# A hybrid attention block on one core: order of loading the first value weights, order of the late value tiles, and place of three steps of the state chains

## The chip, the core and the metric

The kernel runs on one core of one Trainium2 chip. A core has five engines with queues of their own: TensorE (PE; its weight loads are listed apart, as PEld), VectorE (DVE), ScalarE (ACT), GpSimd (POOL) and SyncE (SP), which here only issues DMAs. The metric is the device time of one execution in microseconds; a time is the median over the runs.

## The reference

One layer of a bidirectional hybrid encoder on x of 1024 tokens by 1024 features, in float32:

```python
h = rmsnorm(x, norm_mix)
q, k, v, r, lr_f, lr_b, u, g_a, g_b = jnp.split(h @ w_in, split_points, axis=-1)
log_a_f = jax.nn.log_sigmoid(lr_f @ w_decay_up_fwd + b_decay_fwd) / 16      # log_a_b alike
o = gla_chunked(q, k, v, log_a_f, True) + flip(gla_chunked(flip(q), flip(k), flip(v), flip(log_a_b), False))
o = per_head_rmsnorm(o) * gla_norm * silu(r)
y_a = o @ w_branch_gla
y_b = pooled(u) @ w_pool_group * pool_scale
x = x + (sigmoid(g_a) * y_a + sigmoid(g_b) * y_b) @ w_out
x = x + swiglu(rmsnorm(x, norm_ffn)) ; out = rmsnorm(x, norm_final)
```

The gated linear attention has 4 heads with keys of 128 and values of 256 columns. In each direction a state of 128 x 256 runs over the chunks of tokens: `S_t = diag(alpha_t) S_(t-1) + k_t^T v_t`. This recurrence is the chain that the change touches; the other part of the change is at the start, where x is normalized and the first products with `w_in` are made.

## The kernel before

**Products.** Float32 operands are split into a high part (a cast to fp32r on ScalarE) and a low part (a subtraction on VectorE or GpSimd; `split_to`, L196 to L198). A product of two split operands is three matmuls: high with high, high with low, low with high (`products`, L268; all its matmuls are listed under L271). `mm3` (L273) is such a product followed by `pump`, which advances work that runs beside.

**Work beside.** The order of all engines' instructions is the order in which the program emits them; each engine takes its own in that order. Side work is written as generators in the list `side`; `begin(gen, delay)` (L186) appends one. `pump(dt)` (L158) takes `dt` from the first generator's delay (1 for an `mm3` of 512 columns, 0.5 for one of 256) and advances it when the delay is spent; a `yield d` in it means "after d more". Only the first generator of the list advances. `finish_side` (L189) drains the list at once. `pending` holds splits of weights, `take` (L256) hands out the next projection weights and `prepare` (L248) starts the splits of those after; `prepare_beside` paces a second list of side work.

**Memory.** `slot()` gives one of 39 slots of 128 x 1024 float32. The pool `wts` has a tag `raw` with four buffers for weights as they are loaded. Five PSUM banks (`ps_g`) serve transposes and attention, three (`ps_mm`) the main products. A tile that is given a buffer waits until the former tile's readers are done.

**Start.** SyncE issues the loads of x tiles 0 and 1, small vectors, four of the eight weight tiles of the values of heads 0 and 1 ("pair weights", `vraw`, each 128 x 512), x tiles 2 and 3, and the low-rank weights (`lraw`). The other four pair weights are issued by `split_pair_weight` (L368), each when the split before has freed a buffer. `norm_x(t)` (L390) normalizes tile t (a Square with a sum on ScalarE, the power on GpSimd, the scaling on VectorE) and issues the load of tile t + 4 into the same slot. `to_features` (L332) transposes two tiles on TensorE and splits them into `hT` (hh and hl). `pair_products(ts)` (L439) makes the values of heads 0 and 1 for token tiles ts; the first call, for tiles 0 and 1, is interleaved with `first_steps(k)` (L452), which splits the weights for step k + 1, transposes and norms. Tiles 2 and 3 follow, with norms and transposes of tiles 4 and 5 beside, then `first_qk` (L887): the low-rank product (`low_rank`, L479), q and k of head 0, with norms and transposes of tiles 6 and 7 beside. Values of tiles 4, 5 and then 6 with 7 are made after `begin(attention(0, ...))` (L909), so beside the attention of head 0.

**Attention of a head** (generator `attention`, L665), beside the products of what comes next. For each half of the tokens and each direction: `decay` sums the logarithms (VectorE, with a scan), `exponentials` (ScalarE, three Exp), `apply_decay` (ke on VectorE, qe and a factor on GpSimd). `transposed_keys` (L748) transposes ke on TensorE and splits it into kt. The backward chain (L814 to L830) goes over the eight chunks from the last down: `advance` (L756) makes kv = k^T v on TensorE (three matmuls), the new state st = kv * factor + old on VectorE, and the next step's old state so = st * factor on VectorE; then ScalarE writes the state for this chunk's output, sb. Chunks 7 to 4 use kt of the upper half, 3 to 1 that of the lower. `scores(0)` (sc) follows, then the forward chain (L836 to L863): per chunk the output op from scores and values, from qe and sb, and from qe and sf (ScalarE's scaled state), with `advance` between. `while h not in v_heads` (L805) holds the chain until the values of the head are made.

Of the kernel before, what the change touches and what calls it, by code (L numbers as in the profile page):

```python
# [10 lines left out]
F32 = mybir.dt.float32  # L11
# [3 lines left out]
AF = mybir.ActivationFunctionType  # L15
ALU = mybir.AluOpType

P = 128
D = 1024
SEQ = 1024  # L20
KT = D // P
NT = SEQ // P
HALF = 512
HEADS = 4
DK = 128
DV = 256
# [25 lines left out]
def kernel(  # L52
# [38 lines left out]
    def name(s):  # L91
        count[0] += 1
        return f"{s}_{count[0]}"
# [92 lines left out]
    def begin(gen, delay=0.0):  # L186
        side.append([gen, delay])

    def finish_side():  # L189
        while side:  # L190
            for _ in side[0][0]:
                pass
            side.pop(0)


    def split_to(hi, lo, src, eng=nc.vector):  # L196
        nc.scalar.copy(hi, src)  # L197
        eng.tensor_tensor(lo, src, as_f32(hi), op=ALU.subtract)  # L198
# [133 lines left out]
    def to_features(xn, t0, act, gain):  # L332

        for kp in range(KT // 2):
            ps = bank(ps_g, "tr")
            for i in range(2):
                transpose_tile(ps, xn[i], i, kp)
            gain_and_split(ps, kp, t0, act, gain)
            yield 1
# [10 lines left out]
    def load_x(t):  # L350
        nc.sync.dma_start(xt[t % 4][:, :], x[t * P : (t + 1) * P, :])
# [7 lines left out]

    pair_raw, pair_w = [], []  # L360

    def load_pair_weight():
        k = len(pair_raw)
        raw = wts.tile([P, HALF], F32, tag="raw", name=name("vraw"), bufs=4)
        nc.sync.dma_start(raw[:, :], w_in[k * P : (k + 1) * P, V0 : V0 + 2 * DV])
        pair_raw.append(raw)

    def split_pair_weight():  # L368
        k = len(pair_w)
        w = slot(F32R, s="wv")  # L370
        pair_w.append((w[:, 0, :], w[:, 1, :]))
        split_to(*pair_w[k], pair_raw[k][:, :], (nc.vector, nc.gpsimd)[k % 2])
        if len(pair_raw) < KT:
            load_pair_weight()

    load_x(0)
    load_rows(0, *vec_rows[0])
    load_x(1)
    for i in range(1, len(vec_rows)):
        load_rows(sum(n for _, n in vec_rows[:i]), *vec_rows[i])  # L380
    for _ in range(4):
        load_pair_weight()
    for t in (2, 3):
        load_x(t)
    nc.sync.dma_start(lraw[:, :, :], w_in[:, LR0:U0].rearrange("(k p) c -> p k c", p=P))
    nc.gpsimd.memset(uraw[:, :, :, :], 0.0)

# [8 lines left out]
    def norms(t0):  # L396
        for t in (t0, t0 + 1):
            norm_x(t)
            yield 2
# [13 lines left out]
    def low_rank_weights():  # L413
        for i in range(2):
            raw = lraw[:, 4 * i : 4 * i + 4, :]
            nc.scalar.copy(lw[i][:, :, :3, :], raw.unsqueeze(2).broadcast_to([P, 4, 3, 2 * RANK]))
            nc.vector.tensor_tensor(lw[i][:, :, 3, :], raw, as_f32(lw[i][:, :, 0, :]), op=ALU.subtract)
        nc.scalar.copy(up[:, :, :, :], uraw[:, :, :, :])
        nc.vector.tensor_tensor(up[32:64], uraw[32:64], as_f32(up[32:64]), op=ALU.subtract)
# [19 lines left out]
    def pair_products(ts, before=None):  # L439
        banks = [bank(ps_mm) for _ in ts]  # L440
        for k in range(KT):
            if before:
                before(k)
            for ps, t in zip(banks, ts):
                mm3(ps[:, :], tokens(hT(k, t // 4), t), pair_w[k], k == 0, k == KT - 1)
        for ps, t in zip(banks, ts):
            for h in range(2):
                if t % 4 == 0:
                    pair_v[h].append((slot(F32R, (4, DV), "vh"), slot(F32R, (4, DV), "vl")))
                split_to(*(part[:, t % 4, :] for part in pair_v[h][t // 4]), ps[:, h * DV : (h + 1) * DV])  # L450

# [18 lines left out]
    pair_products((2,))  # L470
    finish_side()
    begin(to_features(xn, 4, hT, g_mix), 1)
    low_rank_weights()
    prepare()
    pair_products((3,))
    finish_side()
    lrT = slot(F32R, (2, HALF), "lrT")

    def low_rank(half):  # L479
# [185 lines left out]
    def attention(h, q, k):  # L665
# [71 lines left out]
        def factor(n, d, which):  # L737
            f = fac[n // 4, d]
            i = n % 4
            if which == "whole":  # L740
                return f[:, 8 + i : 9 + i]
            first_half = (which == "before") == (d == 0)
            return f[:, 2 * i : 2 * i + 1] if first_half else f[:, 2 * i + 1 : 2 * i + 2]
# [9 lines left out]
            split_to(kt[:, 0, :], kt[:, 1, :], kp[:, :])  # L753
            return kt

        def advance(old, n, d, kt):  # L756

            kv = bank(ps_g, "kv")
            products(kv[:, :DV], tokens((kt[:, 0, :], kt[:, 1, :]), n), value(n))
            new = s1((DV,), "st")[:, :]  # L760
            after = factor(n, d, "after")
            if old is None:
                nc.vector.tensor_scalar(new, kv[:, :DV], after, None, op0=ALU.mult)
            else:
                nc.vector.scalar_tensor_tensor(
                    new, kv[:, :DV], after, old[:, :], op0=ALU.mult, op1=ALU.add
                )
            following = n + 1 if d == 0 else n - 1
            old = s1((DV,), "so")
            nc.vector.tensor_scalar(old[:, :], new, factor(following, d, "whole"), None, op0=ALU.mult)  # L770
            return new, old

        def scores(half):
            sc = [bank(ps_g, "sc") for _ in range(2)]
# [26 lines left out]
        yield 1.5  # L801
        apply_decay(0, 0)
        decay(1, 0)
        yield HOLD
        while h not in v_heads:  # L805
            yield 0.5
        v = v_heads[h]
# [4 lines left out]
        sb = [slot(shape=(4, DV), s="sb") for _ in range(2)]  # L812
        old = None
        for n in range(NT - 1, 0, -1):  # L814
            state, old = advance(old, n, 1, kts[n // 4, 1])
            m = n - 1
            nc.scalar.activation(
                sb[m // 4][:, m % 4, :], state, AF.Copy, scale=factor(m, 1, "before")
            )
            if n == 7:  # L820
                exponentials(1, 0)
            elif n == 5:
                apply_decay(1, 0)
            yield 1.2
            if n == 7:
                kts[0, 1] = transposed_keys(0, 1)
                yield 0.5
            if n == 2:
                kts[0, 0] = transposed_keys(0, 0)
                yield 0.5  # L830
# [5 lines left out]
        for n in range(NT):  # L836
            half, i = n // 4, n % 4
            op = bank(ps_g, "op")
            products(op[:, :DV], tokens(p, n), value(n), last=False)
            terms = []  # L840
            if n < NT - 1:
                terms.append((chunk_of(qe, n, 1), sb[half][:, i, :]))
            if n > 0:
                terms.append((chunk_of(qe, n, 0), sf[:, :]))
            for j, (a, b) in enumerate(terms):
                if j == len(terms) - 1 and n < NT - 1:
                    state, old = advance(old, n, 0, kts[half, 0])
                    sf = s1((DV,), "sf")
                    nc.scalar.activation(sf[:, :], state, AF.Copy, scale=factor(n + 1, 0, "before"))
                nc.tensor.matmul(op[:, :DV], a, b, start=False, stop=j == len(terms) - 1)  # L850
            nc.vector.tensor_copy(o[half][:, i, :], op[:, :DV])
            nc.scalar.activation(
                op[:, DV:], op[:, :DV], AF.Square, scale=1.0 / 16.0, accum_out=ms[:, n : n + 1]
            )
            if n == 0:
                yield 0.38
                kts[1, 0] = transposed_keys(1, 0)
            if n == 1:
                yield 0.75
                q_next = scores(1)  # L860
            if n == 3:
                p = q_next
            yield 1.02  # L863
# [22 lines left out]

    def first_qk():  # L887
        q, k = slot(s="q"), slot(s="k")
        begin(norms(6), 1)
        low_rank(0)  # L890
        weights = [take()]
        begin(to_features(xn[2:], 6, hT, g_mix), 1)
        for half in range(2):
            if half:
                finish_side()
                low_rank(1)
                prepare()
            for n, (dst, scale) in enumerate(((q, DK**-0.5), (k, 1.0))):
                if n == len(weights):
                    weights.append(take(ahead=False))  # L900
                ps = feature_major(weights[n], hT, half)
                nc.scalar.activation(dst[:, half, :], ps[:, :], AF.Copy, scale=scale)
        return q, k

    for h in range(HEADS):
        qk = project_qk() if h else first_qk()
        begin(attention(h, *qk))
        if h == 0:
            for ts in ((4,), (5,), (6, 7)):  # L909
                pair_products(ts)  # L910
            v_heads.update(enumerate(pair_v))
            prepare_beside(map(branch_jobs, range(4)), 5)
        if h > 1:
            v = value_slots()
            w = take()
            for t in range(NT):
                values(w, v, t)
            v_heads[h] = v
# [1009 lines left out]
```

## Time and profile before

| what | us |
|---|---|
| median of 3 runs (lowest, highest) | 1404.41 (1403.36, 1405.44) |
| the profiled execution, its own time | 1404.11 |
| its span, first to last instruction | 1402.4 |
| TensorE busy | 1367.1 |
| VectorE, GpSimd, ScalarE busy | 857.7, 744.3, 624.6 |
| mean granted TensorE clock | 0.998 |

In a timeline row stand: start and duration in us, engine, line, operation, written tile, then the tiles read, shapes, the count of merged instructions, and in brackets the idle time of the engine before it with what ended that idle time. A row of waits has the total, the number and the longest of them. In a group of instructions stand the count, the busy time, the mean in ns, and the idle time before them. TensorE's durations overlap in a row of matmuls; its pace is read from the starts. Rows of SPq are DMAs as they are issued, not as they land.

### The profile page before, as it was taken

What the parts mean: (1) busy time and instruction counts of PE and PEld (TensorE: products, weight loads), DVE (VectorE), ACT (ScalarE), POOL (GpSimd) and SP (SyncE); (2) the same over time, 40 slices, a digit from 0 to 9 for tenths busy, and PEclk for the clock granted to TensorE, in tenths of its full rate; (3) what the DMA queues carried; (4) which work ended last, traced back from release to release, by engine and by line L of the source; (5) the groups of instructions that cost most, each with busy time, mean ns of one, the idle gap of its engine ahead of it and who ended that gap; (6) DMA issues with size and microseconds to landing.
All of it is one profiled execution on the core that took longest, in us unless ns stands there. A gap on an engine that the chain in (4) does not pass through costs nothing. (4 is left out here: it accounts for less than half of the span.)

```text
span 1402.4 us, 18182 instructions
## 1 busy us (share of the span) xinstructions
PE 1367.1 (97%) x6485; PEld 1143.3 (82%) x6485; DVE 857.7 (61%) x1076; ACT 624.6 (45%) x1119; POOL 744.3 (53%) x555
## 2 busy tenths in 40 slices
PE   6999999999999999999999999999999999999997
PEld 5778898988888878788887888888888888888876
DVE  5456667676934975577884865656555556343363
ACT  5545646554433444455346633333333334453253
POOL 3212526242279455567666076667666667464354
PEclk9999999999999999999999999999999999999999
DMA  6111324132469757997524555554444447976451
GB/s 214 39 45 49 115 63 143 52 121 61 135 188 279 223 194 231 347 405 264 182 88 161 183 182 173 173 172 149 138 149 148 139 155 254 386 258 222 166 229 72
DMA packets 166588, 243.61 MB, mean 174 GB/s; under 512 B 10937, under 2 KB 95969, under 8 KB 166497
## 3 DMA queue, kind: packets, MB, share of 16 engines
q1 hardware_dynamic: 166496, 242.45, 51.5%
q8 instruction: 51, 0.84, 0.3%
q14 instruction: 41, 0.33, 0.1%
HBM read 164.55 MB, written 77.86 MB: 173 GB/s over the span
## 5 line engine op out<-in xcount | busy, mean ns | idle before, releaser
L198 POOL TENSOR_TENSOR wl<-fs,wh 128x512 fp32r<-128x512 f32 x120 | 166.0, 1387 | 164.3 <-ACT wh L197 139.0
L271 PE MATMUL ps<-gl,wh 128*128 128x512 f32 x616 | 239.8, 389 | 0.9 <-DVE gl L1520 0.9
L271 PE MATMUL ps<-gh,wh 128*128 128x512 f32 x616 | 240.3, 390 | 0.0
L271 PE MATMUL ps<-gh,wl 128*128 128x512 f32 x616 | 239.7, 389 | 0.0
L198 POOL TENSOR_TENSOR wl<-fraw,wh 128x512 fp32r<-128x512 f32 x90 | 129.6, 1441 | 64.8 <-ACT wh L197 64.7
L271 PE MATMUL ps<-hh,wh 128*128 128x512 f32 x376 | 151.6, 403 | 0.0
L198 POOL TENSOR_TENSOR ol<-gor,oh 128x1024 fp32r<-128x1024 f32 (+1 forms) x42 | 100.0, 2386 | 93.2 <-ACT oh L197 76.0
L271 PE MATMUL ps<-hh,wl 128*128 128x512 f32 x376 | 146.7, 390 | 0.0
L271 PE MATMUL ps<-hl,wh 128*128 128x512 f32 x376 | 146.5, 390 | 0.0
L271 PEld LDWEIGHTS ps<-gl,wh 128*128 128x128 f32 x616 | 115.6, 188 | 25.0 <-DVE gl L1520 1.3
L271 PEld LDWEIGHTS ps<-gh,wl 128*128 128x128 f32 x616 | 115.6, 188 | 24.2
L271 PEld LDWEIGHTS ps<-gh,wh 128*128 128x128 f32 x616 | 115.6, 188 | 23.6
L198 POOL TENSOR_TENSOR wl<-raw,wh 128x512 fp32r<-128x512 f32 x40 | 54.4, 1370 | 129.5 <-ACT wh L197 119.1
L271 PE MATMUL ps<-oh,oh 128*128 128x512 f32 x308 | 119.9, 389 | 1.0 <-DVE x L1850 1.0
L271 PE MATMUL ps<-ol,oh 128*128 128x512 f32 x308 | 120.0, 389 | 0.2 <-DVE ol L198 0.2
L271 PE MATMUL ps<-oh,ol 128*128 128x512 f32 x308 | 119.8, 389 | 0.0
L198 POOL TENSOR_TENSOR wl<-wraw,wh 128x512 fp32r<-128x512 f32 x56 | 89.6, 1629 | 45.3 <-ACT wh L197 45.2
L198 DVE TENSOR_TENSOR ol<-wor,oh 128x1024 fp32r<-128x1024 f32 (+1 forms) x42 | 62.0, 1496 | 53.6 <-ACT oh L197 46.3
L197 ACT CAST wh<-fs 128x512 fp32r<-128x512 f32 x120 | 73.7, 615 | 28.3 <-DVE fs L940 28.2
L271 PEld LDWEIGHTS ps<-hh,wl 128*128 128x128 f32 x376 | 70.6, 188 | 15.1
L271 PEld LDWEIGHTS ps<-hl,wh 128*128 128x128 f32 x376 | 70.8, 188 | 13.0
L271 PEld LDWEIGHTS ps<-hh,wh 128*128 128x128 f32 x376 | 70.7, 188 | 13.0
(259 smaller groups left out, 3115.1 us busy)
## 6 DMA issues: line engine op xcount, KB each, us to landing
fraw<-in_w_ffn_in_dram SPq DMA_DIRECT2D x44, 512.0 KB, 5.8
gor<-g_out SPq DMA_DIRECT2D x35, 512.0 KB, 5.5
g_out<-s SPq DMA_DIRECT2D x44, 256.0 KB, 2.3
raw<-in_w_in_dram SPq DMA_DIRECT2D x40, 256.0 KB, 5.2
fraw<-in_w_in_dram SPq DMA_DIRECT2D x20, 512.0 KB, 6.6
wor<-t_out SPq DMA_DIRECT2D x20, 512.0 KB
g_out<-g SPq DMA_DIRECT2D x33, 256.0 KB, 3.2
x<-in_x_dram SPq DMA_DIRECT2D x16, 512.0 KB, 4.9
```

The costliest lines, as they stand in the source:

```text
L197: nc.scalar.copy(hi, src)
L198: eng.tensor_tensor(lo, src, as_f32(hi), op=ALU.subtract)
L271: nc.tensor.matmul(ps, a[i], b[j], start=first and n == 0, stop=last and n == 2, skip_group_check=onto)
```

## The change

All eight pair weights are loaded ahead, two to a slot, between x tiles 2 and 3 and after; the chained loads of `split_pair_weight` go. Norms and transposes of tiles 6 and 7 are begun ahead of the fourth pair product rather than in `first_qk`, and the drain behind that product goes. Late values are made in the order 7, 6, then 5 with 4. In `attention`, the transposed keys of the lower half backward and the exponentials of the upper half forward move from the chain's first step to 2.5 ahead of it, and that half's `apply_decay` from the third step of the chain to its first. `advance` scales both the state for the output and the old state on ScalarE, in this order.

```diff
-    def load_pair_weight():
-        k = len(pair_raw)
-        raw = wts.tile([P, HALF], F32, tag="raw", name=name("vraw"), bufs=4)
-        nc.sync.dma_start(raw[:, :], w_in[k * P : (k + 1) * P, V0 : V0 + 2 * DV])
-        pair_raw.append(raw)
+    def load_pair_weights():
+        raw = slot(s="vraw")
+        for i in range(2):
+            k = len(pair_raw)
+            nc.sync.dma_start(raw[:, i, :], w_in[k * P : (k + 1) * P, V0 : V0 + 2 * DV])
+            pair_raw.append(raw[:, i, :])
...
-        split_to(*pair_w[k], pair_raw[k][:, :], (nc.vector, nc.gpsimd)[k % 2])
-        if len(pair_raw) < KT:
-            load_pair_weight()
+        split_to(*pair_w[k], pair_raw[k], (nc.vector, nc.gpsimd)[k % 2])
...
-    for _ in range(4):
-        load_pair_weight()
-    for t in (2, 3):
-        load_x(t)
+    load_pair_weights()
+    load_pair_weights()
+    load_x(2)
+    load_pair_weights()
+    load_x(3)
+    load_pair_weights()
...
-                if t % 4 == 0:
+                if t // 4 == len(pair_v[h]):
...
     begin(to_features(xn, 4, hT, g_mix), 1)
+    begin(norms(6), 0.5)
+    begin(to_features(xn[2:], 6, hT, g_mix), 2)
     low_rank_weights()
     prepare()
     pair_products((3,))
-    finish_side()
...
-        def advance(old, n, d, kt):
+        def advance(old, n, d, kt, dst):
...
-            nc.vector.tensor_scalar(old[:, :], new, factor(following, d, "whole"), None, op0=ALU.mult)
-            return new, old
+            nc.scalar.activation(dst, new, AF.Copy, scale=factor(following, d, "before"))
+            nc.scalar.activation(old[:, :], new, AF.Copy, scale=factor(following, d, "whole"))
+            return old
...
-        yield HOLD
+        yield HOLD - 2
+        kts[0, 1] = transposed_keys(0, 1)
+        exponentials(1, 0)
+        yield 2.5
...
-            state, old = advance(old, n, 1, kts[n // 4, 1])
             m = n - 1
-            nc.scalar.activation(
-                sb[m // 4][:, m % 4, :], state, AF.Copy, scale=factor(m, 1, "before")
-            )
+            old = advance(old, n, 1, kts[n // 4, 1], sb[m // 4][:, m % 4, :])
             if n == 7:
-                exponentials(1, 0)
-            elif n == 5:
                 apply_decay(1, 0)
             yield 1.2
-            if n == 7:
-                kts[0, 1] = transposed_keys(0, 1)
-                yield 0.5
...
-                    state, old = advance(old, n, 0, kts[half, 0])
                     sf = s1((DV,), "sf")
-                    nc.scalar.activation(sf[:, :], state, AF.Copy, scale=factor(n + 1, 0, "before"))
+                    old = advance(old, n, 0, kts[half, 0], sf[:, :])
...
-        begin(norms(6), 1)
         low_rank(0)
         weights = [take()]
-        begin(to_features(xn[2:], 6, hT, g_mix), 1)
...
-            for ts in ((4,), (5,), (6, 7)):
+            for ts in ((7,), (6,), (5, 4)):
                 pair_products(ts)
```

`HOLD` is 4.4.

## The prediction

> **What bounds the kernel now.** I read the page's busy line first, then the waits of TensorE over the whole span, then busy times by stretch, and last the timeline round the few waits that the change can reach.
>
> ```profile
> PE 1367.1 (97%) x6485; PEld 1143.3 (82%) x6485; DVE 857.7 (61%) x1076; ACT 624.6 (45%) x1119; POOL 744.3 (53%) x555
> ```
>
> TensorE sets the time. The other engines cost time only where TensorE waits, so the change is worth the waits that it ends less those it starts. TensorE's waits, longest first:
>
> ```profile
> PE vps L427 <- DMA rows<-in_b_decay_bwd_dram: 6.7, 1, 6.7
> PE ps L271 <- ACT hh L325: 3.8, 1, 3.8
> PE kv L271 <- DVE kt L198: 3.7, 3, 1.4
> PE tr L318 <- DVE xn L307: 2.4, 3, 1.1
> ...
> PE kv L271 <- ACT vh L197: 1.9, 1, 1.9
> ```
>
> The first is the start of the program and stays. The other four, 11.8 us, lie in the stretch that is edited. Busy times in three stretches (us and, after PEclk, granted clock, DMA share, GB/s) show what else is lost:
>
> ```profile
> core 0: us, PE busy (x) PEld busy (x) DVE busy (x) ACT busy (x) POOL busy (x), PEclk, DMA share, GB/s
> 10.00:20.00 10.00, 6.66 (x29) 5.30 (x27) 3.72 (x6) 4.40 (x11) 2.58 (x2) 1.00 0.87 308
> 20.00:30.00 10.00, 8.63 (x37) 6.76 (x38) 5.87 (x13) 6.30 (x16) 4.35 (x4) 0.83 0.60 168
> 900.00:1000.00 100.00, 100.00 (x443) 82.81 (x442) 51.94 (x56) 35.65 (x64) 63.82 (x47) 1.00 0.47 151
> ```
>
> Undisturbed, 443 matmuls of 512 columns take 100 us: 0.226 us each, though each is listed as 0.39 because they overlap. Right after the long wait the granted clock is 0.83 over 10 us, which is 1.7 us of clock lost.
>
> **Part 1: the pair weights.** The start in order of time:
>
> ```profile
> 6.56 0.90 SPq L351 DMA_DIRECT2D x<-in_x_dram  x2
> 7.51 0.43 SPq L385 DMA_DIRECT2D lraw<-in_w_in_dram  x1
> 8.07 2.51 SPq L351 DMA_DIRECT2D x<-in_x_dram  x2
> 10.57 1.09 PE L271 MATMUL ps<-wv,hh 128*128 128x512 f32 x2
> 10.68 3.83 SPq L365 DMA_DIRECT2D vraw<-in_w_in_dram  x4
> 12.16 0.63 ACT L197 CAST wv<-vraw 128x512 fp32r<-128x512 f32 x1
> 16.27 0.39 PE L271 MATMUL ps<-wv,hl 128*128 128x512 f32 x1
> 18.39 0.62 ACT L197 CAST wv<-vraw 128x512 fp32r<-128x512 f32 x1 [5.60 <-DMA vraw<-in_w_in_dram]
> 20.47 0.73 PE L271 MATMUL ps<-wv,hh 128*128 128x512 f32 x2 [3.81 <-ACT hh L325]
> 22.10 0.80 PE L271 MATMUL ps<-wv,hl 128*128 128x512 f32 x1 [0.90 <-DVE hl L328]
> ...
> 26.56 0.60 PE L318 MATMUL tr<-ident,xn 128*128 128x128 f32 x4
> 26.91 0.71 PE L271 MATMUL ps<-wv,hh 128*128 128x512 f32 x2
> ...
> 30.31 0.70 PE L271 MATMUL ps<-wv,hh 128*128 128x512 f32 x2
> ```
>
> TensorE's 3.81 us are named after ScalarE's hh, but ScalarE itself stood 5.60 us for the fifth weight: its load was issued at 10.68, behind four tiles of x and lraw. In the change x3, lraw, x4 and x5 come behind it: 3 x 128 x 1024 x 4 B and 1024 x 32 x 4 B, 1.70 MB fewer ahead. At the 308 GB/s of that stretch this is 5.5 us, so the weight lands at 18.4 - 5.5 = 12.9, as ScalarE finishes the fourth cast (12.16 + 0.63 = 12.8). From there ScalarE's work runs on without a stop while TensorE has matmuls until 16.5.
>
> How early can the eight steps end? They are 8 x 2 x 3 = 48 matmuls, 10.9 us, plus four groups of transposes at 26.91 - 26.56 = 0.35, 1.4 us: begun at 10.57, they end at 22.9 at best, where now the next product starts at 30.31. 7.4 us are lost: 3.81 + 0.90 idle, most of the 1.7 of clock, the rest small. I take **6.5 us**, leaving 0.9 for the norms of x2 and x3, which now come closer on TensorE's heels (cover: the four steps until 16.5; without it each late norm shows as a wait for hh or hl). Bounds: 3.8 (only the wait for the load goes, and the following steps stay limited by ScalarE and VectorE) to 7.4. SyncE issues the four loads 0.45 us apart (0.90 / 2); x4 and x5 move behind them and are read only after the first product, lraw later still. The weights leave the pool of four raw buffers for four of 39 slots, free at the start, so q's first weights find their buffers free; were slots short, a later tile would wait for a split that is long done.
>
> [...]
>
> **Part 2: norms of tiles 6 and 7 and their transposes earlier.** Of the waits for xn, tile 5's is not touched; tile 7's is:
>
> ```profile
> 44.19 0.67 ACT L197 CAST wh<-raw 128x512 fp32r<-128x512 f32 x1
> ...
> 44.89 0.39 PE L483 MATMUL ps<-hh,lw 128*128 128x512 f32 x1
> ...
> 46.22 1.06 ACT L311 ACTIVATE xn<-x 128x1024 f32<-128x1024 f32 x1
> 49.20 0.38 PE L318 MATMUL tr<-ident,xn 128*128 128x128 f32 x2
> 50.63 0.44 PE L318 MATMUL tr<-ident,xn 128*128 128x128 f32 x2 [1.06 <-DVE xn L307]
> ```
>
> The low-rank product begins at 44.89; its eight pairs take 2 x 0.226 = 0.45 us and count 2/3 each. Before, the norms come with its second and fifth pair, the transposes one product of 0.68 after its last: 49.20. Now the norms come with the sixth and eighth product of the fourth pair product (two products, and none, ahead of 44.89), the transposes with its sixth or seventh pair: norms 2.3 us sooner, transposes 1.1 to 1.6 (47.6 to 48.1 of this clock). ScalarE is busy with earlier work until about 44.9, so the Square starts 1.3 us sooner than 46.22, not 2.3, and the transposes may overtake that. With the transposes 1.1 sooner the wait shrinks a little, with 1.6 it grows by 0.3; but tile 6's norm then no longer shares VectorE with the split of the low-rank result. I take **0.6** (bounds -0.5 and 1.1, the whole wait). The removed drain after the fourth product emptied an almost empty list: nothing.
>
> **Part 3: value tiles 7, 6, 5, 4; keys and exponentials ahead of the chain.** Each head's chain stalls once; the four stalls, and what stands in front of head 1's:
>
> ```profile
> 104.27 0.38 PE L271 MATMUL kv<-vh,kt 128*128 128x256 f32 x1 [1.92 <-ACT vh L197]
> 172.00 0.48 DVE L763 TENSOR_SCALAR st<-kv,fac 128x256 f32<-128x256 f32 x1
> 172.57 0.51 ACT L817 ACTIVATE sb<-st,fac 128x256 f32<-128x256 f32 x1 [4.34 <-DVE st L763]
> 172.59 1.47 DVE L770 TENSOR_SCALAR so<-st,fac 128x256 f32<-128x256 f32 x1
> 175.20 0.69 DVE L198 TENSOR_TENSOR kt<-kp,kt 128x512 fp32r<-128x512 f32 x1 [1.14 <-ACT kt L197]
> 175.95 0.39 PE L271 MATMUL kv<-vh,kt 128*128 128x256 f32 x1 [1.42 <-DVE kt L198]
> 180.78 2.16 PE L778 MATMUL sc<-qe,ke 128*128 128x128 f32 x16
> 240.07 0.39 PE L271 MATMUL kv<-vh,kt 128*128 128x256 f32 x1 [1.20 <-DVE kt L198]
> 302.83 0.39 PE L271 MATMUL kv<-vh,kt 128*128 128x256 f32 x1 [1.06 <-DVE kt L198]
> ```
>
> Head 0's chain starts with tile 7, which is split last; turned round, tile 7 is split two products before. The 1.92 goes. In heads 1 to 3, kt of the lower half is wanted at the fifth step, and its cast on ScalarE stands behind exponentials that stand behind the first sb, which waited 4.34 us for VectorE. Ahead of the chain the cast no longer waits for st; its subtraction follows the decay on VectorE, which ends by 172.0, so kt is there at about 172.8, wanted at 175.95 - 1.42 = 174.5. The 1.42 + 1.20 + 1.06 = 3.68 go. The exponentials now make ScalarE wait for the decay, but it waited there for st anyway; value casts queue behind them as before. Yields: 4.4 + 0.5 become 2.4 + 2.5, so the chain's place does not move.
>
> **Part 4: the old state on ScalarE.** 56 instructions move:
>
> ```profile
> L770 DVE TENSOR_SCALAR so<-st,fac 128x256 f32<-128x256 f32 x56 | 28.2, 504 | 3.7
> ```
>
> On ScalarE such a scaling takes 0.51 (sb above): it gains 56 x 0.51 = 28.6 us, VectorE loses 28.2. A link of the chain was st 0.48 (172.00 above) + so 0.50 = 0.98 (up to 0.48 + 1.47 = 1.95); it becomes st 0.48 + dst 0.51 + old 0.51 = 1.5, with casts in between more. TensorE notices through the banks: I count that sc's second bank is the one of the fifth state. Head 1: st7 172.8, fifth state ready 4 x 1.5 + 0.5 later, 179.3; sc wants the bank halfway through its 2.16, at 180.78 - 1.42 + 1.0 = 180.4. Slack 1 us; about none in heads 2, 3 and 0, where links ran shorter. So I give back 0.4 in head 0 and 0.8 in the others together: **1.5 and 2.9 us** (bounds 0 to 1.9 and -3, one bank wait of 2 us a head over the gain, to 3.7).
>
> [...]
>
> Sum: 6.5 + 0.6 + 1.5 + 2.9 = **11.5 us** off the profiled execution's 1404.11 (its span 1402.4 and 1.7 round it), 1392.6. That execution lies 0.3 below the median of 1404.41, so the forecast is **1393**, its own range 1390 to 1396.
>
> **Rivals.**
> (A) ScalarE's chain becomes the bound: sc or the first op waits in each head. For it: the link of 1.5; against it: st starts sooner than now. The 4.4 us of parts 3 and 4 go and some 1.5 more: 1404.4 - 7.1 + 1.5 = 1399. Chance 0.17.
> (B) ScalarE, not the load, paces the start: x3 lands behind two weights, its norm is late, and 3.8 remain of 6.5: 1396. Chance 0.10.
> (C) The change doesn't do what it says: the fifth weight is still last, since all lie in one queue: part 1 falls away, 1399.5. The order of issue speaks against it. 0.04.
> (D) Slower. The forward chain:
>
> ```profile
> 201.36 0.51 ACT L849 ACTIVATE sf<-st,fac 128x256 f32<-128x256 f32 x1 [1.20 <-DVE st L765]
> 202.82 0.59 PE L850 MATMUL op<-sf,qe 128*128 128x256 f32 x2
> ```
>
> sf is ready 0.95 before its matmul. If queued work on ScalarE (the old state, a square, a cast) makes it 1.5 late, each of 28 steps (7 a head) waits 0.55, 15.4 us: 1393 + 15 = 1408. It decides from 0.95 + 11.5 / 28 = 1.36 us of lateness on. Against it: ScalarE idles 1.20 before sf, more than the 0.51 added. 0.04.
>
> **How the numbers follow.** Forecast 0.65, the four rivals 0.35. The range 1389 to 1399.5 runs from all waits gone (7.4 + 1.1 + 1.9 + 3.7 = 14.1, rounded out) through B and most of A. Faster by over 0.2% (below 1401.6): 0.92; within 0.2%, about what this kernel's measurement cannot tell from none: 0.03; slower: 0.05.
>
> **What would show it.** Part 1: no wait over 1 us between 10 and 25, clock 1.00 there, the third product starting near 24. Part 2: the wait on xn under 1.06 near 42. Parts 3 and 4: no kv wait for vh or kt; instead at most short waits of sc or op on st or p. A wait of op for sf, or of sc in every head, would make the forecast wrong; so would casts of weights that still wait for DMA.

## The result and the profile after

| | before | changed |
|---|---|---|
| median (lowest, highest), 6 runs each, us | 1403.17 (1402.41, 1405.44) | 1395.54 (1394.44, 1396.57) |
| ratio, 95% interval | | 0.9943 (0.993 to 0.9955) |
| profiled execution, its own time | 1404.11 | 1395.00 |
| its span | 1402.4 | 1393.0 |

The change makes the kernel 7.6 us faster by the medians, 9.1 by the two profiled executions. The forecast was 1393. What the median gains depends on the kernel before, which scatters: of its 36 executions recorded beside the experiments, the 14 with a mean granted clock of 0.997 or 0.998 took 1401.6 to 1405.7 us, the other 22 (0.995 or 0.996) 1404.0 to 1408.5, while the changed kernel's twelve (0.998 or 0.999) took 1394.4 to 1396.6. Where the changed kernel was run once more (e9 below), the difference of the medians was 10.5.

The busy line of the page of the changed kernel:

```profile
PE 1366.3 (98%) x6485; PEld 1143.3 (82%) x6485; DVE 830.7 (60%) x1020; ACT 643.6 (46%) x1175; POOL 743.6 (53%) x555
```

VectorE lost 27 us, ScalarE got 19; neither is what the time is made of. TensorE's longest waits in the first 400 us:

```profile
PE vps L428 <- DMA rows<-in_b_decay_bwd_dram: 6.8, 1, 6.8
PE tr L318 <- DVE xn L307: 1.9, 3, 1.0
PE op L271 <- ACT p L197: 1.2, 2, 0.6
PE op L271 <- DVE p L198: 0.9, 4, 0.2
```

The waits for hh (3.8), hl (0.9), kt (3.7) and vh (1.9) of before are gone; those of op for p, 2.1 together (0.2 in before), stand in their place. The two stretches of the start, with the columns shown for before:

```profile
10.00:20.00 10.00, 10.00 (x41) 8.28 (x40) 7.25 (x14) 8.57 (x19) 5.92 (x6) 1.00 1.02 350
20.00:30.00 10.00, 10.00 (x54) 8.34 (x53) 5.84 (x15) 6.08 (x15) 1.16 (x2) 1.00 0.61 171
```

TensorE is busy throughout, with 41 and 54 matmuls where there were 29 and 37. The timeline of the start:

```profile
10.64 1.20 PE L271 MATMUL ps<-wv,hh 128*128 128x512 f32 x2
12.07 1.05 PE L271 MATMUL ps<-wv,hh 128*128 128x512 f32 x2
13.34 0.63 PE L271 MATMUL ps<-wv,hh 128*128 128x512 f32 x2
13.42 0.62 ACT L197 CAST wv<-vraw 128x512 fp32r<-128x512 f32 x1 [0.56 <-DMA vraw<-in_w_in_dram]
...
20.86 0.60 PE L318 MATMUL tr<-ident,xn 128*128 128x128 f32 x4
...
39.16 0.39 PE L485 MATMUL ps<-hh,lw 128*128 128x512 f32 x1
43.47 0.44 PE L318 MATMUL tr<-ident,xn 128*128 128x128 f32 x2 [0.74 <-DVE xn L307]
```

The fifth cast comes at 13.42 (before at 18.39), after 0.56 us of waiting for its load. The transposes ahead of the third pair product start at 20.86 instead of 26.56, the low-rank product at 39.16 instead of 44.89.

To see where the gain arises, the starts of the same matmuls in both traces are set against each other; each row is the difference of this trace or that of an experiment below to the profiled execution of before, in us, at the transposes of the third product (26.56 in before), the first product behind both low-rank halves (z, 77.67), the last op of head 0 (139.26) and of head 3 (332.05), and the end of the last matmul (1395.63):

| kernel | third product | behind low-rank | end of head 0 | end of head 3 | last matmul |
|---|---|---|---|---|---|
| changed | -5.70 | -6.03 | -7.65 | -9.20 | -9.38 |
| changed, second trace (e9) | -5.52 | -5.84 | -7.44 | -8.87 | -8.65 |
| loads alone (e4) | -6.07 | -6.08 | -6.05 | -6.73 | -5.03 |
| tile order alone (e5) | -0.82 | -0.81 | +0.21 | -0.19 | -0.43 |
| keys and exponentials alone (e6) | +0.06 | +0.06 | -0.43 | -4.49 | -4.68 |
| old state on ScalarE alone (e3) | -1.15 | -1.15 | -0.79 | +2.04 | +3.06 |
| changed, old state on VectorE (e1) | -5.86 | -6.18 | -8.16 | -11.62 | -12.15 |
| changed, old state first on ScalarE (e2) | -5.67 | -5.98 | -8.60 | -12.96 | -12.49 |
| e2 with later transposes (e7) | -4.98 | -6.75 | -9.37 | -14.01 | -14.24 |
| e7 with a later norm (e10) | -6.48 | -7.88 | -10.49 | -15.30 | -15.18 |
| weights ahead of x (e8) | -4.61 | -4.91 | -6.54 | -7.51 | -6.53 |

So the change won 5.7 in the start, 0.3 behind it, 1.6 in head 0 and 1.55 in heads 1 to 3; the forecast had 6.5, 0.6, 1.5 and 2.9. Each trace is one execution, so differences of some tenths between them mean little: e4 gains 0.68 in heads 1 to 3, where it has no edit. In e3, e4 and e8 some 0.7 to 0.9 us are lost late, between 526 and 759, where nothing was edited: TensorE waits there for the load of ph, 1.8, 0.7 and 0.6 us, which it does not in the trace of before. In e4 a further 0.8 goes near the end.

### The profile page after: what moved, and what is told of

Same layout as the page of the kernel before. It is cut to its first block, busy times and chain, and to the rows that moved or that the text cites. A ratio compares the mean times of both kernels' runs of the same rounds, so it can differ in the third digit from the quotient of the medians.

```text
span 1393.0 us, 18153 instructions
## 1 busy us (share of the span) xinstructions
PE 1366.3 (98%) x6485; PEld 1143.3 (82%) x6485; DVE 830.7 (60%) x1020; ACT 643.6 (46%) x1175; POOL 743.6 (53%) x555
```

## The experiments

Each run's ratio, and what it is said to be below the kernel before by the medians, goes by executions of the kernel before on the same chip.

**The theory after the result.** The waits that the forecast named are the ones that went; heads 1 to 3 gave back more than forecast because the old state sits on ScalarE behind the output's state (a longer link). Rivals: the new order of keys and exponentials itself costs; or the old state on ScalarE costs as such, wherever it stands in its queue. For the start: the half pace of the first matmuls, or the norms that are now close on TensorE's heels.

**Loads alone (e4_only_loads).** The kernel before with the new order of loads:

```diff
-    for _ in range(4):
-        load_pair_weight()
-    for t in (2, 3):
-        load_x(t)
+    load_pair_weights()
+    load_pair_weights()
+    load_x(2)
+    load_pair_weights()
+    load_x(3)
+    load_pair_weights()
```

> The kernel before with only the loads of the pair weights as in the change (all ahead, two to a slot). Theory: the third pair product starts 5.7 us sooner, near 24.6 instead of 30.31, and all of it arrives: 1397 to 1398. Of the 6.5 expected 0.9 is lost since TensorE's clock is at half until 13.3 us here and until 11.4 in the trace of before: where that edge falls elsewhere, the start moves by half of its shift. Rival: the start's gain is partly lost behind, norms of tiles 4 to 7 on TensorE's heels: under 5 us, 1399.

Measured: 1399.88 us, ratio 0.996 (0.9946 to 0.9973), 5.7 below the kernel before by the medians, as its theory had it. The start gains 6.07, and the heads keep their waits. Part 1 stands alone: it does not need the other parts.

**Tile order alone (e5_only_tiles).** The kernel before with:

```diff
-                if t % 4 == 0:
+                if t // 4 == len(pair_v[h]):
...
-            for ts in ((4,), (5,), (6, 7)):
+            for ts in ((7,), (6,), (5, 4)):
```

> The kernel before with one edit: the late value tiles of a head are made in the order 7, 6, then 5 with 4. Theory (as predicted): the wait of kv for vh in head 0, 1.92 us, goes and nothing takes its place, so 1.5 to 2 us less than the kernel before; the three waits of kv for kt (3.7 together), the start and heads 1 to 3 stay as they are. Rival: the chain that is let go earlier in head 0 stops at another place (an op or sc that waits for values or for p), and less than 0.7 us is left of it.

Measured: 1404.03 us, ratio 0.9987 (0.9978 to 0.9997), 1.8 below the kernel before by the medians (0.4 to 3.1 by the interval). That is the size that the theory gave, but its reason fails: something does take the wait's place. The rival's short gain is what the profiled execution shows (0.43 at the last matmul), at a place that the rival did not name. The waits of kv, and the timeline of head 0's chain:

```profile
PE kv L271 <- DVE kt L198: 5.0, 4, 1.8
```

```profile
105.28 0.51 ACT L817 ACTIVATE sb<-st,fac 128x256 f32<-128x256 f32 x1 [0.94 <-DVE st L763]
...
106.18 0.59 ACT L724 ACTIVATE z<-z 128x512 f32<-128x512 f32 x1
...
107.29 0.58 ACT L197 CAST kt<-kp 128x512 fp32r<-128x512 f32 x1
...
108.65 0.39 PE L271 MATMUL kv<-vh,kt 128*128 128x256 f32 x1 [1.80 <-DVE kt L198]
```

Four waits for kt instead of three: the wait for vh is gone (none is listed), and head 0 now stops at the fifth step, as heads 1 to 3 do, for the kt whose cast stands behind sb and the exponentials. In before, head 0 did not show that wait because it had already stood for vh: there this kt was ready at 109.40 and wanted at 110.12. The wait of 1.80 was also followed by 3.41 us at half clock (last section), so this execution loses 1.02 in head 0. Whether the edit pays by itself stays open between the medians and this trace; its wait is gone for good only together with the next edit.

**Keys and exponentials alone (e6_only_ahead).** The kernel before, with the old state left on VectorE and:

```diff
-        yield HOLD
+        yield HOLD - 2
+        kts[0, 1] = transposed_keys(0, 1)
+        exponentials(1, 0)
+        yield 2.5
...
-                exponentials(1, 0)
-            elif n == 5:
                 apply_decay(1, 0)
...
-            if n == 7:
-                kts[0, 1] = transposed_keys(0, 1)
-                yield 0.5
```

> The kernel before with one edit: transposed keys of the lower half backward and exponentials of the upper half forward ahead of the chain, that half's decay at the first step; the old state stays on VectorE. Theory: the three waits of kv for kt, 3.7 us, go without anything in their place, so 3.0 to 3.7 us less than the kernel before, all of it in heads 1 to 3 (about 1.2 each). Then what was lost of this part in the changed kernel was lost to the old state on ScalarE alone. Rival: the order itself costs, the part comes back as waits of op on p or of sc on st, and 2 us or less are gained here too.

Measured: 1400.04 us, ratio 0.9956 (0.994 to 0.9973), 5.8 below the kernel before by the medians, more than the 3.0 to 3.7 expected; the traces put it at 4.68 at the last matmul. In heads 1 to 3 it gains 4.49 - 0.43 = 4.06, a little more than the 3.68 of the waits. Of its waits in the heads are left:

```profile
PE kv L271 <- ACT vh L197: 1.5, 1, 1.5
PE sc L778 <- DVE st L765: 0.5, 1, 0.5
PE op L271 <- DVE p L198: 0.2, 1, 0.2
```

No wait for kt, and one new one, sc's 0.5 (op's 0.2 is there in before too). The order costs next to nothing, and the rival (2 us or less) falls.

**The old state on ScalarE alone (e3_only_scalar_old).** The kernel before, with `advance` as in the change:

```diff
-            nc.vector.tensor_scalar(old[:, :], new, factor(following, d, "whole"), None, op0=ALU.mult)
-            return new, old
+            nc.scalar.activation(dst, new, AF.Copy, scale=factor(following, d, "before"))
+            nc.scalar.activation(old[:, :], new, AF.Copy, scale=factor(following, d, "whole"))
+            return old
```

> The kernel before with only the old state moved to ScalarE. Theory: nothing of the start, vh and kt waits goes (3.8, 1.9, 3.7 us), and longer links make p and sc wait: slower than 1403.2 by 1 to 4 us, 1404 to 1407. Rival: freed of scalings of up to 1.47 us, VectorE makes kt and st sooner, and the kt waits shrink: 1401 to 1403.

Measured: 1408.45 us, ratio 1.0019 (1.0006 to 1.0031): slower. Its waits:

```profile
PE kv L271 <- DVE kt L198: 5.1, 3, 1.8
...
PE op L271 <- DVE p L198: 0.7, 3, 0.2
PE op L271 <- ACT p L197: 0.6, 2, 0.4
```

In heads 1 to 3 it loses 2.04 + 0.79 = 2.83: 1.4 because the cast of kt, still behind the chain's start on ScalarE, comes later (5.1 instead of 3.7), the rest mostly because p does (op's waits are 1.3 here and 0.2 in before). Set beside e6, 4.06 - 2.83 = 1.2, near the 1.55 of the changed kernel.

**The old state back on VectorE (e1_old_vector).** The changed kernel with one line changed:

```diff
-            nc.scalar.activation(old[:, :], new, AF.Copy, scale=factor(following, d, "whole"))
+            nc.vector.tensor_scalar(old[:, :], new, factor(following, d, "whole"), None, op0=ALU.mult)
```

> The changed kernel with the old state scaled on VectorE again; its other three parts stay. Theory: in the changed kernel the links of the backward chain take 1.46 us (st 0.48, dst and old on ScalarE 0.98), so the first state but one ends late, copy_predicated and p behind it, and TensorE waits for p at the first op of every head (0.2 to 0.6 us, with restarts some 3 us in four heads). With links near 0.9 these waits go: 1393 to 1394 against 1395.5, no op wait for p over 0.3. Rival: beside GpSimd VectorE's scaling takes up to 1.47 (mean 0.50 before), and links are as long as now: 1395.5 to 1398, the waits stay.

Measured: 1393.32 us, ratio 0.9913 (0.99 to 0.9927); its slowest execution (1394.11) is below the fastest of the changed kernel's twelve (1394.44). Heads 1 to 3 gain 11.62 - 8.16 = 3.46 instead of 1.55, so most of what they gave back came with this one line. That much fits both the longer link and a ScalarE that is too full; the next run tells them apart.

**The old state first on ScalarE (e2_old_first).** The changed kernel, the two scalings of the backward direction in the other order:

```diff
-            nc.scalar.activation(dst, new, AF.Copy, scale=factor(following, d, "before"))
-            nc.scalar.activation(old[:, :], new, AF.Copy, scale=factor(following, d, "whole"))
+            parts = [(dst, "before"), (old[:, :], "whole")]
+            for to, which in parts if d == 0 else parts[::-1]:
+                nc.scalar.activation(to, new, AF.Copy, scale=factor(following, d, which))
```

> The changed kernel with ScalarE scaling the old state ahead of sb in the backward direction; forward as it is. Theory: a link becomes st 0.48 + old 0.51 + handover, near 1.05 instead of 1.46, six links end 2.4 us sooner, p comes in time: 1393 to 1394, op waits for p at most 0.3. Rival: p is late because ScalarE's queue holds casts (kt, weights, values) ahead of it, not for the links: 1395.5 as now, waits of 0.6 stay.

Measured: 1392.33 us, ratio 0.9908 (0.9894 to 0.9921). Heads 1 to 3 gain 12.96 - 8.60 = 4.36: with the same 56 scalings on ScalarE the loss is gone (e6, with VectorE's, gains 4.06 there), so it is the place in the queue, not the engine. The chain of head 3 in the changed kernel:

```profile
295.14 0.48 DVE L767 SCALAR_TENSOR_TENSOR st<-kv,fac,so 128x256 f32<-128x256 f32 x1 [0.98 <-ACT so L773]
295.66 0.51 ACT L772 ACTIVATE sb<-st,fac 128x256 f32<-128x256 f32 x1 [0.55 <-DVE st L767]
296.08 0.49 ACT L773 ACTIVATE so<-st,fac 128x256 f32<-128x256 f32 x1
296.61 0.48 DVE L767 SCALAR_TENSOR_TENSOR st<-kv,fac,so 128x256 f32<-128x256 f32 x1 [0.98 <-ACT so L773]
...
300.48 0.69 DVE L198 TENSOR_TENSOR kt<-kp,kt 128x512 fp32r<-128x512 f32 x1 [1.93 <-ACT kt L197]
301.09 0.47 DVE L767 SCALAR_TENSOR_TENSOR st<-kv,fac,so 128x256 f32<-128x256 f32 x1
301.48 0.69 DVE L786 COPY_PREDICATED sc<-keep,sc 128x512 f32<-128x512 uint8 x1
302.41 0.56 ACT L197 CAST p<-sc 128x512 fp32r<-128x512 f32 x1
303.02 0.38 PE L271 MATMUL op<-vh,p 128*128 128x256 f32 x1 [0.62 <-ACT p L197]
```

and with the old state first:

```profile
293.49 0.48 DVE L767 SCALAR_TENSOR_TENSOR st<-kv,fac,so 128x256 f32<-128x256 f32 x1 [0.64 <-ACT so L774]
294.55 0.48 DVE L767 SCALAR_TENSOR_TENSOR st<-kv,fac,so 128x256 f32<-128x256 f32 x1 [0.58 <-ACT so L774]
...
297.97 0.69 DVE L787 COPY_PREDICATED sc<-keep,sc 128x512 f32<-128x512 uint8 x1
298.96 0.56 ACT L197 CAST p<-sc 128x512 fp32r<-128x512 f32 x1
300.09 0.28 PE L271 MATMUL op<-vh,p 128*128 128x256 f32 x1
```

A link goes from st to st by way of so. Behind sb it takes 296.61 - 295.14 = 1.47, ahead of it 1.06. Five links make 2 us at the end of the chain. From the sixth st to the last it is 3.03 in both traces: ScalarE casts the forward chain's kt behind the sixth so, VectorE stands 1.93 for that cast, and the last st comes behind kt, late by what the links before it were late. VectorE takes the mask of the scores (COPY_PREDICATED) behind the last st; the cast of p waits for the mask, and the first op for p: it stands 0.62 in the one, and in the other p is ready at 299.52 and op starts at 300.09 without a wait.

**Weights ahead of x (e8_weights_first).** The changed kernel with all eight weights issued ahead of x tiles 2 and 3:

```diff
     load_pair_weights()
     load_pair_weights()
-    load_x(2)
     load_pair_weights()
-    load_x(3)
     load_pair_weights()
+    load_x(2)
+    load_x(3)
```

> The changed kernel with all eight pair weights issued ahead of x tiles 2 and 3 (in the change x2 is issued after four of them, x3 after six). Theory: the start is paced by what lands when; x2 lands behind four more weights of 256 KB, about 3 us later at some 350 GB/s, its norm is late, a wait of ps for hh or hl of more than 1 us appears near 16 to 20, and the time is 1.5 to 3 us above that of the changed kernel (about 1397 to 1398.5 where the kernel before takes 1403.2). Rival: ScalarE's row of casts is the pace and the place of x2 and x3 among the loads makes no difference: the changed kernel's time within 0.5 us.

Measured: 1397.12 us, ratio 0.9934 (0.9919 to 0.9949), 2.1 above the median of the changed kernel on the same chip (e9). The start loses 1.1 against the changed kernel's first trace. The time is as the first theory had it, and so is the chain of causes, though the wait at its end is far smaller than the 1 us that it named:

```profile
15.22 1.06 ACT L311 ACTIVATE xn<-x 128x1024 f32<-128x1024 f32 x1 [1.58 <-DMA x<-in_x_dram]
18.42 0.50 PE L271 MATMUL ps<-wv,hl 128*128 128x512 f32 x1 [0.15 <-DVE hl L328]
```

ScalarE stands 1.58 us for x2's load and begins tile 2's Square at 15.22, in the changed kernel at 13.95 without a wait. The hl behind that norm comes late, and TensorE's starts lie 0.54 apart there (17.88 to 18.42) and 0.52 at 21.61 behind tile 3's norm, instead of 0.23: some 0.6 of the 1.1. Another 0.7 of the 2.1 is the late loss between 526 and 759, where nothing was edited.

**The changed kernel once more (e9_after_again).** No edit.

> The changed kernel as it is, once more. Question: full clock came at 13.32 in its first trace and at 11.40 in that of before. Theory: clock changes fall on a grid of 3.41 us whose place differs from execution to execution, whatever the loads; full clock comes at any time between 10.2 and 13.7, most likely not at 13.3 again, and all that follows the start shifts by no more than half of the difference, since the norms then hold the start back. Rival: the new loads set it; full clock comes between 12.8 and 13.5 again, as in three of four traces with the new loads below the best version. In both cases the time stays 9 to 11 us below that of the kernel before.

Measured: 1394.99 us, ratio 0.9927 (0.9913 to 0.9941), 10.5 below the kernel before by the medians. The matmuls take their full pace from 11.36 on (starts 0.22 to 0.24 us apart; the two ahead of it took 0.95 together), so the rival falls. (Of earlier traces with the new loads the changed kernel's first and e8's come to full pace at 13.34 and 13.53, e7's has it at its first product, 10.72.) Yet the start ends no sooner, because of what these rows of its timeline show:

```profile
18.41 1.29 POOL L198 TENSOR_TENSOR wv<-vraw,wv 128x512 fp32r<-128x512 f32 x1
18.48 1.77 DVE L307 TENSOR_SCALAR xn<-x,n1rs 128x1024 f32<-128x1024 f32 x1 [0.67 <-POOL n1rs L303]
20.17 0.86 DVE L328 SCALAR_TENSOR_TENSOR hl<-tr,cols,hh 128x256 fp32r<-128x256 f32 x2
20.70 0.50 PE L271 MATMUL ps<-wv,hl 128*128 128x512 f32 x1 [1.00 <-DVE hl L328]
```

A TensorE that is earlier runs into the hl of the seventh step, which stands on VectorE behind the scaling of tile 3.

**Later transposes (e7_late_transposes).** The kernel of e2 with:

```diff
-    begin(to_features(xn, 4, hT, g_mix), 1)
     begin(norms(6), 0.5)
-    begin(to_features(xn[2:], 6, hT, g_mix), 2)
+    begin(to_features(xn, 4, hT, g_mix), 1)
+    begin(to_features(xn[2:], 6, hT, g_mix), 1)
```

> The changed kernel with the old state ahead of the output's state on ScalarE in the backward chain (as in e2_old_first), and with the norms of tiles 6 and 7 begun ahead of the transposes of tiles 4 and 5, which so come later. Theory: the waits of the transposes for xn that are left (2.1 us in e2_old_first) are there because these transposes are placed too early, with nothing else wrong; they go, and the time is some 2 us below that of e2_old_first against the kernel before of the same chip, that is some 15 us less than the kernel before (ratio about 0.989). Rival: ScalarE and VectorE are late as such in this stretch; then the waits move to the products that read the split transposes (ps waits for hh or hl) or to the low-rank product, and the time is that of e2_old_first (ratio about 0.991).

Measured: 1390.0 us, ratio 0.9885 (0.987 to 0.9899), 15.8 below the kernel before by the medians, where e2 had 13.3. Its waits in the start:

```profile
PE ps L271 <- DVE hl L328: 1.1, 1, 1.1
PE tr L318 <- DVE xn L307: 0.5, 2, 0.3
PE ps L271 <- POOL wl L198: 0.5, 1, 0.5
```

The waits for xn fall from 2.1 to 0.5, and behind the start 1.77 are gained instead of e2's 0.31, so what was wrong with these transposes was mainly that they were placed too early. In this trace too the clock was early (the first pair of matmuls, at 10.72, takes 0.71, in the changed kernel's first trace 1.20) and the wait of e9 for hl appeared, 1.1; it takes back part of the gain. It is not the rival's sign, since e9 has it without this edit; the 0.5 for wl, which is new, may be.

**A later norm (e10_norm_later).** The kernel of e7 with tile 3's norm one step later, behind the hl of that step:

```diff
-        if k in (3, 5):
-            norm_x(k // 2 + 1)
+        if k in (3, 6):
+            norm_x(k // 3 + 1)
```

> The kernel of e7_late_transposes with the norm of tile 3 one step later in the first product, behind the hl of the sixth step instead of ahead of it. Theory: the wait of ps for hl there (1.1 us, with a scaling of xn of 1.77 instead of 0.75 on VectorE ahead of hl, beside a split on GpSimd) goes, and xn is still ready for its transposes; 0.5 to 1.1 us less than e7_late_transposes. Rival: xn comes later by as much, and the wait moves to the transposes of tile 3 (tr waits for xn, about 1 us): no difference within 0.4 us, or up to 1 us more.

Measured: 1389.27 us, ratio 0.989 (0.9875 to 0.9906), not to be told from e7 by the ratios. Its timeline shows the step that was meant:

```profile
18.09 0.86 DVE L328 SCALAR_TENSOR_TENSOR hl<-tr,cols,hh 128x256 fp32r<-128x256 f32 x2
19.87 0.75 DVE L307 TENSOR_SCALAR xn<-x,n1rs 128x1024 f32<-128x1024 f32 x1 [0.86 <-POOL n1rs L303]
20.68 0.44 PE L318 MATMUL tr<-ident,xn 128*128 128x128 f32 x2 [0.22 <-DVE xn L307]
```

hl comes at 18.09 instead of 20.17 (e9), xn is there 0.22 after its transposes ask for it, and the wait of 1.1 is gone. With full pace from the first product on (its first pair, at 10.69, takes 0.70), this is the one trace in which the start gains 6.48. This kernel and e7 are the best of those run, each some 16 us below the kernel before on its chip (1405.46 - 1389.27; 1405.83 - 1390.0).

## Why the prediction was right, and where it was off

The result lies in the forecast's range, 2.5 us above its value, and the waits that went are the ones named. Of the sum of 11.5 the traces show 9.2 up to the end of head 3: the terms for the start, for tiles 6 and 7 and for heads 1 to 3 were too large, and that of head 0 came out by luck. The sum also rests on one execution of the kernel before that had a clock of 0.998; in most others the clock was lower, and the 10.5 of e9's medians is nearer to the forecast partly because the kernel before lost clock that the sum did not count.

**Part 1** (6.5, measured 5.7; 5.5 in the second trace). The step "so the weight lands at 18.4 - 5.5 = 12.9" held within 0.5: the cast came at 13.42, after 0.56 of waiting. The two long waits and the half clock behind them vanished, as said (the granted clock reads 1.00 from 20 to 30, in before 0.83). What was mis-sized is the 0.9 us left "for the norms of x2 and x3, which now come closer on TensorE's heels": together with the half pace at the start they took 1.7 to 1.9. In the first trace the first matmuls ran at half pace until 13.34 (12.07 to 13.34 for three, 0.42 each instead of 0.226), in the second only until 11.36, and TensorE then stood 1.00 for hl. The cover that the prediction named, TensorE's matmuls until 16.5, covers tile 2's norm; tile 3's stands in VectorE's queue ahead of an hl that the same product needs. Only with that norm later and full pace from 10.69 (e10) the start gains the 6.5. In the first trace no wait was left there, so what a shorter one does to the clock was not put to the test here; in e5 one of 1.80 was followed by 3.41 us at half clock (last section).

**Part 2** (0.6, measured 0.3). The wait for tile 7 shrank from 1.06 to 0.74. Measured from the start of the low-rank product, the Square of tile 6 came 1.50 sooner (46.22 - 44.89 = 1.33 behind it in before, 0.17 ahead of it now; forecast 1.3) and the transposes 1.13 (49.20 - 44.89 = 4.31 before, 3.18 now; forecast 1.1 to 1.6). So the transposes did not overtake the norm, and the wait shrank by about the difference, as "shrinks a little" had it; the 0.6 taken was more than these two figures give. That the better edit was to hold the transposes back was not seen; e7 shows it.

**Part 3** (all four kv waits go). Shown: none is left, and e6 by itself gains 4.06 in heads 1 to 3. The step "Head 0's chain starts with tile 7" and so "The 1.92 goes" is true only with the keys ahead: e5 alone lets head 0 wait 1.80 for kt. The prediction did not ask of this wait what is late next.

**Part 4** (give-back 0.8 in heads 1 to 3, measured 4.06 - 1.55 = 2.5). The link was forecast at 1.5 and measures 1.47. The link that it replaces was taken as 0.98 with the mean scaling of 0.50; that mean mixes a median of 0.35 with a few of up to 1.49, so most links were shorter. The failing step is "TensorE notices through the banks": sc stands little (its 16 matmuls take 2.25 in head 3 and 1.95 in e2). The lateness of all five links arrives behind it, at the mask of the scores, and from there at p and the first op. The term was too small by about those waits of op (1.2 + 0.9, less the 0.2 of before and the 0.2 in head 0), and rival A was right on where the price would fall, though not on its size: the forecast had "some 1.5" for all heads on top of the whole of parts 3 and 4 lost, and more than half of these was kept. In head 0 the term came out (1.5, measured 1.6) by two errors that cancel. The trace of e2, with the same tiles and keys and the short links, gains 8.60 - 5.98 = 2.62 there: the end of the wait is worth more than its 1.92, and the long links gave back 1.0, not 0.4. Part of the difference is that TensorE did not run on at once behind this wait: in before the kv matmuls start 0.52 and 0.22 apart behind it (104.27, 104.79, 105.01), and 0.12 apart at the next step (106.96, 107.08, 107.20).

**The rivals.** C is out (e4). D did not happen: the waits hold none of op for sf. Of B came the late norm of tile 3, on VectorE, not ScalarE, and at 1.0 us (e9); 5.5 to 5.7 remained, not 3.8. The long links of VectorE (up to 1.95) vanished: four links in a row of head 3 take 1.45 to 1.47. But those long links had not been what the chain cost: e1, with the old state's scaling on VectorE again, beats the changed kernel, and e6, where these scalings take 0.52 on the mean and single ones in head 3 up to 1.13, gains 4.06 in heads 1 to 3.

## What to carry to other kernels

Where a wait is taken away, look up in the same queue what would have been late just after it: in e5 and in the start the next wait was already there, hidden by the first. A scaled copy that feeds the next link of a chain goes ahead of one that only feeds an output, and the price of a longer link is looked for at the last reader behind the chain (here the mask), not at the first. If a matmul waits for work that is only placed too near, moving its consumer back can be worth as much as moving the work forward.

## What the runs showed of the hardware

**The clock.** In the trace of before the granted clock changes at 11.40, 21.64 and 25.05, which lie 10.24 and 3.41 us apart, three times 3.41 and once. Where the changes lie differs from execution to execution: full clock came at 13.32 in the changed kernel's first trace, and in its second (e9) the starts are at full pace from 11.36 on. Ahead of 13.32 the column of the granted clock reads 1.00 in that first trace, although the matmuls start 0.42 apart (0.226 at full pace); the pace is the better witness there. Not every wait cost clock as well. These are stretches of 3.41 us, first of before (the end of the long wait, and the stretch behind it), then of e5 (the wait of 1.80 in head 0), then of e4:

```profile
18.22:21.64 3.42, 0.73 (x2) 0.30 (x2) 1.58 (x4) 3.25 (x7) 0.83 (x2) 1.00 0.08 31
21.64:25.05 3.41, 2.95 (x7) 2.39 (x8) 2.74 (x7) 2.44 (x6) 2.60 (x3) 0.50 0.50 154
```

```profile
106.65:110.06 3.41, 1.61 (x10) 1.29 (x10) 1.98 (x5) 2.26 (x7) 1.26 (x1) 1.00 0.05 9
110.06:113.48 3.42, 3.42 (x14) 2.73 (x12) 3.17 (x5) 0.97 (x2) 2.82 (x3) 0.50 0.44 119
```

```profile
94.77:98.18 3.41, 1.48 (x7) 0.90 (x5) 2.87 (x6) 0.65 (x2) 0.00 (x0) 1.00 0.54 164
98.18:101.60 3.42, 3.25 (x18) 2.68 (x19) 1.67 (x5) 1.94 (x6) 0.00 (x0) 1.00 0.00 0
```

The stretch with TensorE busy for 0.73 us and that with 1.61 were each followed by one at half clock, 1.7 us lost. In before, the wait of 1.92 in head 0 lay across two stretches (TensorE busy for 2.21 from 100.14 to 103.56 and for 2.57 from 103.56 to 106.97) and cost no clock: both and the next one read 1.00. But e4's stretch, busy for 1.48, was followed by full clock. So the busy time alone does not sort them, as far as the modelled ends of matmuls can tell. That the time of the kernel before scatters because its waits of 1 to 4 us cost clock in some executions and not in others is the author's estimate; only the profiled executions show where the clock changed. The wait of 3.81 of before lay from 16.66 to 20.47, and neither stretch that it touches was idle throughout: TensorE was busy for 1.85 from 14.81 to 18.22 and for 0.73 in the next, and half clock came only behind the second.

**VectorE and GpSimd.** The scaling of tile 3 took 1.77 us where GpSimd's split had started 0.07 ahead of it (e9; the split took 1.29), and 0.75 where it started first; then the split was the long one (1.83), in the changed kernel's first trace:

```profile
19.14 0.75 DVE L307 TENSOR_SCALAR xn<-x,n1rs 128x1024 f32<-128x1024 f32 x1 [0.67 <-POOL n1rs L303]
19.21 1.83 POOL L198 TENSOR_TENSOR wv<-vraw,wv 128x512 fp32r<-128x512 f32 x1
```

With 0.07 us of order the other way VectorE's scaling took 1.0 us more and GpSimd's split 0.5 less, in e9 on TensorE's path.
